# Values and output gate of an mLSTM as one projection of seven block products, in a two-layer hybrid decoder

## The chip, the core and the metric

The kernel runs on one core of a Trainium2 chip. A core has five engines with queues of their own that meet at semaphores: TensorE (matrix products; its weight loads are listed apart as PEld), VectorE (DVE), ScalarE (ACT), GpSimd (POOL) and SyncE (SP), which here only issues loads. DMAs are also issued by POOL, and those of POOL can add to what is already in the destination. Accumulation is in PSUM, eight banks of 128 partitions x 512 numbers; everything else lives in SBUF.

The metric is the device time of one execution in microseconds (us), the median over runs. A measurement here tells a difference of about 0.2% from none.

## What is computed

Two layers over 512 tokens of width 1024. Each has a mixer of two branches and an MLP. Cut to what matters:

```python
def hybrid_layer(x, ...):
    h = rmsnorm(x, norm_mix)
    z = h @ w_in
    q_a, k_a, v_a, q_m, k_m, v_m, o_m, if_m, gates = jnp.split(z, splits, axis=-1)
    q_a = partial_rope(rmsnorm(q_a...)); k_a = partial_rope(rmsnorm(k_a...))
    att = sliding_window_attention(q_a, k_a, v_a, att_sinks)          # 8 heads, 2 key heads, window 128
    hm = mlstm_chunkwise(q_m, k_m, v_m, i_pre, f_pre)                 # 4 heads, values of 128
    hm = rmsnorm(hm, m_head_norm) * jax.nn.sigmoid(o_m)
    g_a, g_m = jnp.split(gates, 2, axis=-1)
    mixed = sigmoid(g_a) * (att @ w_att_branch) + sigmoid(g_m) * (hm @ w_m_branch)
    x = x + mixed @ w_out
    u = relu(rmsnorm(x, norm_ffn) @ w_ff1)
    return x + (u * u) @ w_ff2
```

The edit concerns `v_m` and `o_m`, each `h` (512 x 1024) times 512 columns of `w_in`.

## The kernel before

**Numbers in two parts.** Every operand of a large product is split into a high part (ScalarE copies it into a rounded type) and a low part (VectorE subtracts). `mm3` then makes three matmuls per tile: high by high, high by low, low by high. A group of steps (`group_steps`) computes 512 x 512 outputs: for each 128 rows k of the weight, `chunk` loads a 128 x 512 tile and splits it, and four steps m make three matmuls each into four banks of PSUM. In `feat_steps` the weight is stationary, in `tok_steps` the activation (`acts[k]`, the two parts of the normed, transposed input).

**The order.** The mixer's second half is one list: `weave(fill, side)` (line 819). `fill` is the sequence of projection steps, each a quarter of a unit, so that a group over k = 8 is eight units and one of the branches' groups (k = 4) is four. `side` holds everything else with a place in units: it is traced when the fill reaches that place. Before: the mLSTM's queries and keys (units 0 to 8), gate groups `s0` and `s1` (8 to 24), the values `tok_steps(..., ev_v)` (24 to 32), the attention branch `a_steps(0)`, `a_steps(1)` (32 to 40), gate group `s2` (40 to 48), the output gate `tok_steps(..., ev_o)` (48 to 56), `s3` (56 to 64). Behind the list come the mLSTM's branch on `hmT`, the merge, and `w_out`.

Tracing order is not yet the engines' order: a scheduler puts each engine's instructions into a queue by when they become ready and by priority, and what stands under `tc.high_priority()` (weight loads, their splits, the reading of PSUM) goes ahead. Buffers of one tag are handed out in the order of the trace, though: a tile waits for the release of the one that held its buffer before. Tags that matter: `wraw` (three raw weights), `wh` and `wl` of pool `wsp` (four split weights), `a` of pool `act` (32 tiles of 128 x 512, `slot()`), `t` of pool `tmp` (17, `temp()`), `m` (five banks of PSUM for projections, `bank()`), `aux` (three for everything else), and single ones in `mid`: `mid6` (the attention's values `v2`), `kvi` (its keys), `mid10` (first `kT`, then the mLSTM's values `vm`).

**The side work.** Attention unit i = (block of 128 queries b, key head kv): scores and masks (`att_scores`) at 7 + 1.65 i, softmax (`att_softmax`, exponentials in line 614, scaling in 619) at 1.25 more, transposes, split and POOL's mask (`att_probs`, line 634) at 3.45 more, output at 5.65 more (`att_out`, whose last steps, lines 652 and 653, write block b of `att_acts[2 kv]` and `att_acts[2 kv + 1]`). The last one, i = 7, stands at 24.2. The gates' sigmoids (line 686) follow the reading of their banks; `back` reloads the table of exponentials. mLSTM head h: decay rows (`m_decay`) at 28 + 4.65 h, then four blocks of weights (`m_weights`: exponentials, POOL's mask, a score matmul, a product) and four of outputs (`m_out`, whose matmuls are `aux<-vm,t`). `m_norm` norms all heads, `ev_o` multiplies with the output gate, `head_tr` transposes and splits them into `hmT`.

The MLP of both layers already uses a scheme of seven block products, with sums of activations made by VectorE and sums of weights made by adding DMAs; the mixer's projections are plain.

Of the kernel before, what the change touches and what calls it, by code (L numbers as in the profile page):

```python
# [33 lines left out]
def hybrid_kernel(ctx, tc, x, norm_mix, w_in, att_q_norm, att_k_norm, att_sinks, m_gate_bias,  # L34
# [41 lines left out]
    def temp(dt=F32):  # L76
        return now["tmp"].tile([P, T], dt, tag="t", name=nm("t"))
# [20 lines left out]
    def f32(ap):  # L98
        return ap.bitcast(F32)
# [288 lines left out]
    def mixer(l, norm, late, order, phase):  # L388
# [8 lines left out]
        def wcols(c0, n):  # L397
            return lambda k: [W[k * P:(k + 1) * P, c0:c0 + n]]
# [285 lines left out]
        def sigmoid(tiles):  # L684
            for t in tiles:
                i = sc.activation(t, t, AF.Sigmoid)
            return i

        def back(i):

            with tc.issue_after(i.ins):
                sc.preload_act_table_set(LN_EXP)
# [9 lines left out]

            return sg, feat_steps(acts, wcols(C_G + 512 * g, 512), ev)

        vm = []

        def ev_v(b, ps):
            if b == 0:
# [34 lines left out]
        def m_weights(h, s):  # L743
            cmb = cmbs[h]
            n = (NB - s) * P
            e = wts[h, s] = temp()

            ve.tensor_scalar(e[:, 0:P], cmb[:, s * P:(s + 1) * P], bias[:, s, s, h:h + 1], None, op0=ALU.max)
            sc.activation(e[:, 0:P], e[:, 0:P], AF.Exp, scale=-1.0, bias=bias[:, s, s, h:h + 1])
            for t in range(s + 1, NB):  # L750
                eb = e[:, (t - s) * P:(t - s + 1) * P]
                sc.activation(eb, cmb[:, t * P:(t + 1) * P], AF.Exp, scale=-1.0,
                              bias=bias[:, s, t, h:h + 1])
            gp.affine_select(out=e[:, 0:P], in_=e[:, 0:P], compare_op=ALU.is_ge, fill=0.0,
                             base=0, pattern=[[1, P]], channel_multiplier=-1)
            ps = aux()
            ks = slice(s * P, (s + 1) * P)
            pe.matmul(ps[:, :n], m_k[h][:, ks], m_q[h][:, s * P:], start=True, stop=False)
            pe.matmul(ps[:, :n], m_k[h][:, ks], m_ql[h][:, s * P:], start=False, stop=True)
            ve.tensor_tensor(e[:, :n], e[:, :n], ps[:, :n], op=ALU.mult)  # L760

        def m_out(h, t):
            ps = aux([P, MV + 1])
            for s in range(t + 1):
                pe.matmul(ps, wts[h, s][:, (t - s) * P:(t - s + 1) * P], vm[0][:, s, h, :],
                          start=s == 0, stop=s == t)
            dn = sm([P, 1], "dn")
            ve.scalar_tensor_tensor(dn, ps[:, MV:], -1.0, em[:, t, h:h + 1], op0=ALU.mult, op1=ALU.max)
            ve.tensor_tensor(dn, ps[:, MV:], dn, op=ALU.max)
            ve.reciprocal(dn, dn)  # L770
            hs = hm[t][:, h * MV:(h + 1) * MV]
            sc.activation(hs, ps[:, :MV], AF.Copy, scale=dn)
            sc.activation(ps[:, :MV], hs, AF.Square, accum_out=hss[:, t, h:h + 1])

        def m_norm():
            ve.tensor_scalar(hss, hss, 1.0 / MV, EPS, op0=ALU.mult, op1=ALU.add)
            hr = sm([P, NB, MH], "hr", 1)
            rsqrt(hr, hss, "hq")
            for t in range(NB):
                h3 = hm[t].rearrange("p (h v) -> p h v", h=MH)  # L780
                ve.tensor_tensor(h3, h3, hr[:, t, :].unsqueeze(2).to_broadcast([P, MH, MV]), op=ALU.mult)

        prod = []

# [9 lines left out]
        def ev_o(b, ps):  # L794
            so = temp()
            sc.activation(so, ps, AF.Sigmoid, scale=norm.col[:, b:b + 1])
            ve.tensor_tensor(hm[b], hm[b], so, op=ALU.mult)
            if b == NB - 1:
                sigmoid(g2)

        for h in range(MH):
            at = 28 + 4.65 * h
            side.append((at, lambda h=h: m_decay(h)))
            for i in range(NB):
                side += [(at + 1.75 + 4.65 * i / NB, lambda h=h, i=i: m_weights(h, i)),
                         (at + 4.65 + -0.55 + 4.65 * (i + 0.5) / NB, lambda h=h, i=i: m_out(h, i))]
# [564 lines left out]
```

## Time and profile before

| | |
|---|---|
| device time, median of 3 runs | 1304.13 us (1303.62 to 1304.37) |
| span of the profiled execution | 1302.9 us |
| mean granted TensorE clock over the span | 1.000 |
| bytes moved by DMA | 177.61 MB, mean 136 GB/s |

The profile lists for each engine its busy time as a share of the span. Matmuls are pipelined, so their own durations (about 389 ns for 512 columns) overlap; the distance from one start to the next is what one costs. A line such as L47 is that of the helper through which all matmuls go, so matmuls are told apart by their tiles: `mm<-...` are projections, `aux<-...` attention and mLSTM. Other tiles: `i` parts of the input, `a` a tile of `act`, `t` one of `tmp`, `w`, `wh`, `wl` a weight and its parts.

### The profile page before, as it was taken

To read this page: it belongs to the slowest core of one execution; us is meant where nothing else is said; L and a number is where in the kernel's file an instruction comes from. 1 tells how busy PE (TensorE), PEld (TensorE's weight loads), DVE (VectorE), ACT (ScalarE), POOL (GpSimd) and SP (SyncE) were. 2 spreads that over 40 slices of the span, in tenths; PEclk is the share of its full clock that TensorE was granted. 3 is DMA by queue.
4 is the path that set the end of the run, shared out by engine and by line. 5 is a ranking of instruction groups with operands and counts; after the bars stand their busy time and mean duration, and the time that the engine had idled before them with its cause. 6 is when DMAs were issued, how large, how long until landed. Compare 5 with 4: busy or idle time off the path is not lost. (4 is left out here: it accounts for less than half of the span.)

```text
span 1302.9 us, 19074 instructions
## 1 busy us (share of the span) xinstructions
PE 1291.5 (99%) x6978; PEld 1105.2 (85%) x6978; DVE 955.5 (73%) x1505; ACT 763.7 (59%) x1329; POOL 200.4 (15%) x281
## 2 busy tenths in 40 slices
PE   9999999999999999999999999999999999999998
PEld 6877788888889999999888778888888899999987
DVE  4699754475677897968948996545737878879797
ACT  5578755544466665656555787554445556665563
POOL 4511100000003021131115111000000030311210
PEclk9999999999999999999999999999999999999999
DMA  5422222372369888898124222223714597988953
GB/s 154 110 72 59 74 81 74 90 249 82 98 155 172 236 185 207 195 211 216 33 75 114 65 66 75 79 75 92 256 57 129 141 215 195 201 212 196 213 148 98
DMA packets 130542, 177.61 MB, mean 136 GB/s; under 512 B 9864, under 2 KB 78320, under 8 KB 130448
## 3 DMA queue, kind: packets, MB, share of 16 engines
q1 hardware_dynamic: 94208, 131.82, 32.7%
q0 software_dynamic: 35520, 44.17, 21.2%
q8 instruction: 55, 0.90, 0.3%
q10 hardware_dynamic: 720, 0.40, 0.1%
q14 instruction: 39, 0.32, 0.1%
HBM read 174.27 MB, written 2.10 MB: 135 GB/s over the span
## 5 line engine op out<-in xcount | busy, mean ns | idle before, releaser
L47 PE MATMUL mm<-i,wh 128*128 128x512 f32 (+1 forms) x1280 | 352.7, 362 | 0.0
L867 ACT ACTIVATE wh<-raw 128x1024 fp32r<-128x1024 f32 x212 | 223.1, 1056 | 181.1 <-PE mm L47 114.0
L868 DVE TENSOR_TENSOR wl<-raw,wh 128x1024 fp32r<-128x1024 f32 x212 | 255.2, 1218 | 74.2 <-ACT wh L867 72.3
L47 PEld LDWEIGHTS mm<-i,wh 128*128 128x128 f32 x1280 | 224.3, 189 | 32.1 <-DVE a L699 0.8
L166 DVE TENSOR_TENSOR wl<-w,wh 128x512 fp32r<-128x512 f32 (+1 forms) x208 | 140.8, 679 | 137.7 <-ACT wh L165 129.4
L47 PE MATMUL mm<-i,wl 128*128 128x512 f32 (+1 forms) x640 | 229.8, 360 | 0.0
L165 ACT ACTIVATE wh<-w 128x512 fp32r<-128x512 f32 (+1 forms) x208 | 127.0, 611 | 146.7 <-PE mm L47 122.8
L47 PE MATMUL mm<-wh,uh 128*128 128x512 f32 x440 | 171.8, 390 | 0.0
L47 PE MATMUL mm<-wl,uh 128*128 128x512 f32 x440 | 171.7, 390 | 0.0
L47 PE MATMUL mm<-wh,ul 128*128 128x512 f32 x440 | 171.2, 389 | 0.0
L1027 POOL DMA_DIRECT2D raw<-in_w_ff_dram x48 | 62.3, 1304 | 591.3 <-DMA raw<-in_w_ff_dram 316.9
L47 PE MATMUL mm<-wh,i 128*128 128x512 f32 (+1 forms) x512 | 150.6, 370 | 1.2 <-ACT wh L165 0.6
L47 PEld LDWEIGHTS mm<-i,wl 128*128 128x128 f32 x640 | 120.8, 189 | 18.1 <-DVE wl L868 0.4
L47 PEld LDWEIGHTS mm<-wh,i 128*128 128x128 f32 x512 | 92.0, 188 | 19.0 <-DVE i L179 2.1
L913 DVE SCALAR_TENSOR_TENSOR x<-mm,ms,x 128x512 f32<-128x512 f32 x126 | 90.4, 743 | 9.9 <-PE mm L47 9.9
L47 PEld LDWEIGHTS mm<-wh,ul 128*128 128x128 f32 x440 | 82.6, 188 | 17.4
L47 PEld LDWEIGHTS mm<-wh,uh 128*128 128x128 f32 x440 | 82.8, 188 | 16.1
L47 PEld LDWEIGHTS mm<-wl,uh 128*128 128x128 f32 x440 | 82.8, 188 | 15.6
L47 PE MATMUL mm<-wl,i 128*128 128x512 f32 (+1 forms) x256 | 93.0, 363 | 0.0
L47 PE MATMUL mm<-wh,a 128*128 128x512 f32 x256 | 81.3, 392 | 0.0
L47 PE MATMUL mm<-a,wh 128*128 128x512 f32 x256 | 80.5, 397 | 0.0
L47 PE MATMUL aux<-i,wh 128*128 128x256 f32 x384 | 69.5, 283 | 0.0
(259 smaller groups left out, 2161.0 us busy)
## 6 DMA issues: line engine op xcount, KB each, us to landing
raw<-in_w_ff_dram SPq DMA_DIRECT2D x144, 512.0 KB, 5.2
raw<-in_w_ff_dram POOLq DMA_DIRECT2D x84, 512.0 KB, 7.8
w<-in_w_in_dram SPq DMA_DIRECT2D x128, 256.0 KB, 2.6
w<-in_w_out_dram SPq DMA_DIRECT2D x32, 256.0 KB, 2.7
w<-in_w_att_branch_dram SPq DMA_DIRECT2D x16, 256.0 KB, 2.6
w<-in_w_m_branch_dram SPq DMA_DIRECT2D x16, 256.0 KB, 2.7
w<-in_w_in_dram SPq DMA_DIRECT2D x16, 128.0 KB, 2.1
out_dram<-x SPq DMA_DIRECT2D x7, 256.0 KB, 2.0
```

Of the source, the lines that this page charges most:

```text
L47: latest[0] = nc.tensor.matmul(*args, **kw)
L165: sc.activation(wh[:, :off], raw[:, :off], AF.Copy)
L166: ve.tensor_tensor(wl[:, :off], raw[:, :off], f32(wh[:, :off]), op=ALU.subtract)
L867: sc.activation(hi, src, AF.Copy)
L868: ve.tensor_tensor(lo, src, f32(hi), op=ALU.subtract)
L913: ve.scalar_tensor_tensor(xh[:, cc], ps[i][:, cc], ms[j][:, b:b + 1], xh[:, cc], op0=ALU.mult, op1=ALU.add)
L1027: gp.dma_start(to[h], src(h, i, j), accum_op=ALU.add)
```

## The change

The values and the output gate are no longer two groups of 8 x 4 steps. The activation is seen as two halves of tokens by two halves of k, the weight as two halves of k by two column blocks (output gate, values), and the four 256 x 512 results are made of seven products of 256 x 512 x 512 in the manner of Strassen and Winograd. `vo_step(n, k, i)` is one step of product n: three matmuls for rows k and tokens i of a half.

- Products 1, 2 and 4 take activation quarters as they are; 5, 6, 3 and 7 take sums, made by `sums1`, `sums_next` and `sums3` (nine VectorE operations on 128 x 1024 in the bytes of `mid6` and `kvi`, then splits into `tmp` tiles).
- Products 1 and 2 take weight blocks through `chunk`; the others take weight sums in `wa` (`tmp` tiles, begun at unit 25) and `wb` (`act` tiles), loaded by SP and added to by POOL's DMAs (`more`), 16 of them in a layer.
- Results are read from PSUM in between (`value`, `output`); the output gate's sigmoids follow the last product (`gates_o`) with a table reload behind them, and `m_norm` multiplies with them.
- The order becomes: queries and keys, `s0`, `s1`, `a_steps(0)`, `a_steps(1)` (24 to 32), the seven products (32 to 46), `s2`, `s3` (46 to 62).
- The mLSTM starts at 39.6 instead of 28, with 3.2 units from head to head instead of 4.65; `m_norm` stands at 56.9, `head_tr` at 58.4 + f. The sigmoids of `g2` are traced together with those of `g3`.

```diff
+        def more(r, i, j, k):
+            with tc.high_priority():
+                gp.dma_start(r, block(i, j, k), accum_op=ALU.add)
...
+        def begin(k):
+            wa[k] = temp()
+            load(wa[k], 0, 0, k)
+            more(wa[k], 0, 1, k)
+
+        def weight(n, k):
+            if n in (1, 2):
+                return chunk([block(n - 1, 0, k)])
+            if n == 3:
+                wb[k] = slot()
+                load(wb[k], 1, 1, k)
+            w = parts_of((wb if n in (3, 7) else wa)[k])
+            if n == 5:
+                more(wa[k], 1, 1, k)
+            if n == 6:
+                more(wa[k], 1, 0, k)
+            if n == 3:
+                more(wb[k], 0, 1, k)
+            return w
...
+        def sums1():
+            a, b = (mid.tile([P, 4, H], F32, tag=t, name=nm("sc")) for t in ("mid6", "kvi"))
+            scratch["a"], scratch["b"] = a, b
+            (h10, l10), (h11, l11) = quad(1, 0), quad(1, 1)
+            ve.tensor_tensor(a, h10, l10, op=ALU.add)
+            ve.tensor_tensor(b, h11, a, op=ALU.subtract)
+            ve.tensor_tensor(b, b, l11, op=ALU.add)
+            sum_parts(5, b)
+
+        def sums_next(key, t, i):
+            b = scratch["b"]
+            h, lo = quad(t, i)
+            ve.scalar_tensor_tensor(b, b, -1.0, h, op0=ALU.mult, op1=ALU.subtract)
+            ve.tensor_tensor(b, b, lo, op=ALU.subtract)
+            sum_parts(key, b)
...
-            sc.activation(vm[0][:, b, :, 0:MV], ps.rearrange("p (h v) -> p h v", h=MH), AF.Copy,
-                          scale=norm.col[:, b:b + 1])
...
+        def gates_o():
+            for b in range(NB):
+                last = sc.activation(so[b], so[b], AF.Sigmoid, scale=norm.col[:, b:b + 1])
+            back(last)
+
+        plan = {5: ("y", None, [(value, 1, True)]), 1: ("x", (0, 0), [(output, 0, True)]),
+                3: ("y", None, [(value, 0, True)]), 6: ("x", None, [(value, 0, False)]),
+                2: ("f", (0, 1), [(output, 0, False)]), 7: ("x", None, [(value, 1, False), (output, 1, True)]),
+                4: ("f", (1, 1), [(output, 1, False)])}
...
+        def vo_step(n, k, i):
+            which, at, outs = plan[n]
+            fresh = n in (5, 1, 2, 4) and k == 0
+            if fresh and i == 0:
+                held[which] = [bank(), bank()]
+            if i == 0:
+                ready[0] = weight(n, k)
+            if at:
+                c = slice(H * at[0] + i * P, H * at[0] + (i + 1) * P)
+                ah, al = (a[:, c] for a in acts[4 * at[1] + k])
+            else:
+                ah, al = (a[:, k % 2, i * P:(i + 1) * P] for a in sums[n][k // 2])
+            mm3(held[which][i], ah, al, ready[0][0], ready[0][1], fresh, False, skip_group_check=True)
...
+        vo_steps = [(0.25, lambda n=n, k=k, i=i: vo_step(n, k, i))
+                    for n in (5, 1, 3, 6, 2, 7, 4) for k in range(4) for i in range(2)]
...
+                ve.tensor_tensor(hm[t], hm[t], so[t], op=ALU.mult)
...
+        side += [(25.0 + 0.5 * k, lambda k=k: begin(k)) for k in range(4)]
+        side += [(25.0, sums1), (28.5, lambda: sums_next(6, 0, 0)), (31.5, lambda: sums_next(3, 0, 1)), (36.5, sums3)]
+        pace = 3.2
         for h in range(MH):
-            at = 28 + 4.65 * h
+            at = 39.6 + pace * h
...
-        side.append((28 + 4.65 * (MH + 1) + -0.55, m_norm))
+        side.append((56.9, m_norm))
         g2, s2 = gate_steps(2)
-        g3, s3 = gate_steps(3, lambda: back(sigmoid(g3)))
+        g3, s3 = gate_steps(3, lambda: back(sigmoid(g2 + g3)))
...
-        side += [(57.75 + 1.25 * f, lambda f=f: head_tr(f)) for f in range(MH)]
-        weave(feat_steps(acts, wcols(C_QM, 512), ev_qk) + s0 + s1 + tok_steps(acts, wcols(C_VM, 512), ev_v)
-              + a_steps(0, g0) + a_steps(1, g1) + s2 + tok_steps(acts, wcols(C_OM, 512), ev_o) + s3, side)
+        side += [(58.4 + 1.0 * f, lambda f=f: head_tr(f)) for f in range(MH)]
+        weave(feat_steps(acts, wcols(C_QM, 512), ev_qk) + s0 + s1 + a_steps(0, g0) + a_steps(1, g1) + vo_steps
+              + s2 + s3, side)
```

More of the change, by code (lines that the diff above doesn't have):

```diff
@@ new lines, in parts_of @@
+        def parts_of(r):
+            with tc.high_priority():
+                wh, wl = (now["wsp"].tile([P, T], F32R, tag=t, name=nm(t)) for t in ("wh", "wl"))
+                sc.activation(wh, r, AF.Copy)
+                ve.tensor_tensor(wl, r, f32(wh), op=ALU.subtract)
+            return wh, wl
+        def begin(k):
[16 more added lines that the diff above has]
+            return w
@@ new lines, in quad, with sum_parts @@
+        def quad(t, i):
+            return [f32(g[:, :, H * t:H * (t + 1)]) for g in norm.groups[i]]
+        def sum_parts(key, src):
+            sums[key] = [split(src[:, 2 * p:2 * p + 2, :], get=lambda: now["tmp"].tile([P, 2, H], F32R, tag="t", name=nm("t")))
+                         for p in range(2)]
+        def sums1():
[6 more added lines that the diff above has]
+            sum_parts(5, b)
@@ new lines, in output @@
+        def output(t, ps, first):
+            for i in range(2):
+                if first:
+                    so.append(slot())
+                    sc.activation(so[-1], ps[i], AF.Copy)
+                else:
+                    ve.tensor_tensor(so[2 * t + i], so[2 * t + i], ps[i], op=ALU.add)
+        def gates_o():
[6 more added lines that the diff above has]
+                4: ("f", (1, 1), [(output, 1, False)])}
@@ new lines, in mixer @@
+        held, ready = {}, {}
+        def vo_step(n, k, i):
[8 more added lines that the diff above has]
+                ah, al = (a[:, c] for a in acts[4 * at[1] + k])
+            else:
+                ah, al = (a[:, k % 2, i * P:(i + 1) * P] for a in sums[n][k // 2])
+            mm3(held[which][i], ah, al, ready[0][0], ready[0][1], fresh, False, skip_group_check=True)
+            if k == 3 and i == 1:
+                with tc.high_priority():
+                    for f, t, first in outs:
+                        f(t, held[which], first)
+                if n == 4:
+                    gates_o()
```

37 lines of the change are left out of this document (26 added, 11 removed).

## The prediction

> **What bounds the kernel now.** I read the page first, then the chain of waits, then busy time by stretches of the second layer's mixer, and last the timeline of each engine in the 20 us in which the edit takes work away.
>
> ```profile
> span 1302.9 us, 19074 instructions
> ...
> PE 1291.5 (99%) x6978; PEld 1105.2 (85%) x6978; DVE 955.5 (73%) x1505; ACT 763.7 (59%) x1329; POOL 200.4 (15%) x281
> ...
> PEclk9999999999999999999999999999999999999999
> ```
>
> From the chain (start, length, what), and from the stretches (stretch, its length, then each engine's busy time and instructions):
>
> ```profile
> 872.67 20.50 PE mm L47 x90
> ```
>
> ```profile
> core 0: us, PE busy (x) PEld busy (x) DVE busy (x) ACT busy (x) POOL busy (x), PEclk, DMA share, GB/s
> ...
> 136.00:152.00 16.00, 16.00 (x75) 12.80 (x74) 12.55 (x31) 13.76 (x39) 2.91 (x4) 1.00 0.23 68
> 716.00:781.40 65.40, 62.63 (x317) 48.68 (x317) 60.34 (x150) 51.76 (x141) 9.90 (x17) 1.00 0.24 65
> 781.40:797.60 16.20, 16.20 (x75) 12.96 (x74) 12.65 (x33) 13.92 (x40) 2.91 (x4) 1.00 0.23 66
> 808.30:862.50 54.20, 54.20 (x279) 46.10 (x278) 29.19 (x89) 29.89 (x91) 4.36 (x13) 1.00 0.27 77
> ```
>
> TensorE is idle for 11.4 us of 1302.9, so a matmul removed is time removed, and a wait of TensorE is time added. Busy time does not say what a matmul costs, since they overlap; the chain of waits does: 90 in 20.50 us, 0.228 us each. One unit of the woven program (four steps of three matmuls) is 2.73 us. Up to 781.4 us the attention runs beside the first 24 units, and there VectorE is busy 60.34 of 65.40 us: the attention is behind its places in the list, and what is left of it is done in the next 16 us, in which ScalarE is busy 13.92. Layer one shows the same (136 to 152).
>
> That stretch is where the edit acts. Columns: start, length, engine, line, operation, out<-in, shapes, count, idle before.
>
> ```profile
> 781.21 0.39 PE L47 MATMUL mm<-i,wl 128*128 128x512 f32 x1
> 781.43 0.39 PE L47 MATMUL mm<-wh,i 128*128 128x512 f32 x1
> ...
> 789.95 0.63 PE L52 MATMUL aux<-ident,t 128*128 128x128 f32 x4
> 790.33 1.17 PE L47 MATMUL aux<-t,v 128*128 128x512 f32 x4
> ```
>
> ```profile
> 782.26 1.66 ACT L686 ACTIVATE a<-a 128x512 f32<-128x512 f32 x3
> 784.35 0.63 ACT L165 ACTIVATE wh<-w 128x512 fp32r<-128x512 f32 x1 [0.43 <-PE mm L47]
> 785.00 1.28 ACT L692 ACT_TABLE_LOAD   x1
> 786.30 0.40 ACT L614 ACTIVATE t<-t,m 128x128 f32<-128x128 f32 x1
> ...
> 787.12 0.63 ACT L165 ACTIVATE wh<-w 128x512 fp32r<-128x512 f32 x1
> ...
> 790.08 0.61 ACT L165 ACTIVATE wh<-w 128x512 fp32r<-128x512 f32 x1
> ...
> 795.78 0.63 ACT L165 ACTIVATE wh<-w 128x512 fp32r<-128x512 f32 x1 [0.73 <-PE mm L47]
> ```
>
> ```profile
> 791.93 1.00 POOL L634 TENSOR_SCALAR_AFFINE_SELECT t<-t 128x512 fp32r<-128x512 f32 x1 [11.60 <-ACT t L175]
> 793.16 2.11 POOL L634 TENSOR_SCALAR_AFFINE_SELECT t<-t 128x512 fp32r<-128x512 f32 x3 [0.23 <-DVE t L176]
> ```
>
> ```profile
> 789.12 0.68 DVE L619 TENSOR_TENSOR t<-t,den 128x512 f32<-128x512 f32 x1
> ...
> 797.31 0.49 DVE L653 TENSOR_TENSOR a<-t,a 128x128 fp32r<-128x128 f32 x2 [0.17 <-ACT a L652]
> ```
>
> The second gate group ends at 781.43, where the values' projection (stationary `i`) takes over. The seventh attention unit (block 3, first key head) is then still before its softmax: its exponentials start at 786.30, behind the last sigmoids and a table load, line 619 scales them at 789.12, its transposes follow at 789.95, its masks on POOL at 791.9 and 793.2, and its pair of attention parts is complete at about 797.6. TensorE never notices, because 96 matmuls of the values fill the gap.
>
> **The change part by part, for one layer.**
>
> *Matmuls.* Values and gate take 2 x 8 x 4 x 3 = 192 matmuls of 512 columns; seven products take 7 x 4 x 2 x 3 = 168. 24 x 0.228 = **-5.5 us**. Nothing else leaves TensorE.
>
> *The branch behind the first gates.* At unit 24 stands now `a_steps(0)`. Its first matmul needs `att_acts[0]` for all four blocks, hence the seventh unit's parts. Could TensorE do something else meanwhile? The weight parts live in four buffers in program order, so the first branch group holds all four; no later product can be prepared. The new product's sums take the bytes of `v2`, which the last attention unit reads; the mLSTM's tiles come after those. So TensorE waits. When are the parts ready? Before: 797.6. The values' weight passes on ScalarE fall away (784.35 with its wait: 1.08 us to 785.00; 787.12 and 790.08: about 0.53 each, since neighbours overlap by 0.1; the one at 795.78: 0.7): 797.6 - 2.8 = 794.8. From 781.43 that is 13.4 us, of which TensorE works on two sets of transposes (0.38 us from 789.95 to the next row) and two attention outputs (four matmuls of 0.228, 0.91): 2.6. **+10.8 us**. Bounds: no speeding-up, 797.6 - 781.4 - 2.6 = 13.6; and from below, if the softmax started right behind the last sigmoid (783.9, without even a table load) and ran as it did from 786.30 on, less the 2.8: 797.6 - 2.4 - 2.8 = 792.4, 11.0 - 2.6 = 8.4. The second branch pair (eighth unit) is needed 24 matmuls later, 5.5 us, and comes about 2 us later: no wait.
>
> *The clock.* Between 781.8 and about 788 nothing is there for TensorE: over 6 us. What happens then is seen at the program's two ends only:
>
> ```profile
> 1.22 2.93 PE L47 MATMUL aux<-ones 128*128 128x256 f32 x6 [1.22 <-POOL ones L108]
> 5.01 0.94 PE L47 MATMUL aux<-ones 128*128 128x128 f32 x6
> 1298.00:1299.00 1.00, 0.89 (x4) 0.39 (x3) 0.39 (x2) 0.00 (x0) 0.00 (x0) 1.00 0.00 0
> 1301.00:1302.00 1.00, 0.00 (x0) 0.00 (x0) 0.00 (x0) 0.00 (x0) 0.00 (x0) 0.89 0.13 45
> 1302.00:1303.00 1.00, 0.00 (x0) 0.00 (x0) 0.00 (x0) 0.00 (x0) 0.00 (x0) 0.50 0.03 8
> ```
>
> The granted clock falls to 0.50 some 3 us after the last matmul, and the first six matmuls take 2.93 us for 256 columns each, where later six of 128 take 0.94: work is slow from 1.22 to some point between 4.15 and 5.01; I take 3.7 us. If the wait costs the clock, the first 3.7 us behind it run at half speed: 1.8 lost; and one set of transposes and the last output matmuls in the chain take twice as long: 0.6. **+2.4 us**; bounds 0 (the short attention bursts keep it up) and 3.6 (slow for two such times).
> By the Trainium skill (TensorE: Matmul & The Clock Gate, part 1, "The HAM clock gate") one idle window of about 3.4 us halves the clock and about 3.4 us of work restores it, and its advice is to leave no gap over some 3 us between bursts; by that figure the loss is an estimated 1.7 instead of 1.8, and the change breaks the advice twice. The rows at the two ends agree; no gap in the middle of this run is long enough to show it.
>
> *More weights, sums and DMAs.* 28 weight tiles are split instead of 16, 9 operations on 128x1024 and 8 splits of 128x512 make the sums, and 16 loads of 256 KB come with 16 adding DMAs on POOL's queue.
>
> ```profile
> L868 DVE TENSOR_TENSOR wl<-raw,wh 128x1024 fp32r<-128x1024 f32 x212 | 255.2, 1218 | 74.2 <-ACT wh L867 72.3
> L166 DVE TENSOR_TENSOR wl<-w,wh 128x512 fp32r<-128x512 f32 (+1 forms) x208 | 140.8, 679 | 137.7 <-ACT wh L165 129.4
> L1027 POOL DMA_DIRECT2D raw<-in_w_ff_dram x48 | 62.3, 1304 | 591.3 <-DMA raw<-in_w_ff_dram 316.9
> raw<-in_w_ff_dram POOLq DMA_DIRECT2D x84, 512.0 KB, 7.8
> ```
>
> VectorE: 9 x 1.22 + (8 + 12) x 0.68 = 24.6 us, and ScalarE 20 x 0.63 = 12.6; both lie beside 22 units of 2.73 us, 60 us, where VectorE was busy a good half (29.19 of 54.20). POOL: 16 x 1.3 = 21 us at most, in a stretch where it was busy 4.36 of 54.20. An adding DMA of twice the size lands in 7.8 us; each is needed a product or more (8 steps, 5.5 us) later, most two. Queued behind them on POOL are the mLSTM's masks, and at units 25 to 26.5 the attention's last masks. I take **0**; bounds 0 and 3 us (one adding DMA in the way of the masks and one late weight).
>
> *The mLSTM later and closer.* Its last output moves from unit 50.1 to 56.25, and the branch that reads it from 64 to 62.
>
> ```profile
> 864.64 0.48 PE L47 MATMUL mm<-wh,i 128*128 128x512 f32 x1
> ...
> 867.49 0.83 PE L47 MATMUL aux<-vm,t 128*128 128x129 f32 x6
> ...
> 871.61 1.05 PE L47 MATMUL aux<-vm,t 128*128 128x129 f32 x8
> ```
>
> ```profile
> 893.17 0.44 PE aux L52 x4
> ```
>
> ```profile
> 879.81 1.89 DVE L781 TENSOR_TENSOR a<-a,hr 128x512 f32<-128x512 f32 x3
> ...
> 894.37 0.75 DVE L179 SCALAR_TENSOR_TENSOR a<-aux,gcol,a 128x512 fp32r<-128x512 f32 x1 [2.10 <-ACT a L178]
> ```
>
> Unit 48 starts at 864.64 and the last output at 871.61; less 0.6 for the outputs at 867.49 (to the next fill matmul) that is 2.3 units on: 50.3, so it is hardly late. From its end (872.7, where the chain goes on with 90 fill matmuls) to normed heads (881.7) are 9.0 us; four more products by `so`, 0.63 each, 2.5; transposes and split, from 893.17 to 895.12, 1.9: 13.4, with the lateness 0.2 x 2.73 = 0.5 it is 13.9. Cover: 5.75 units, 15.7 us. It just fits; with heads at a distance of 3.2 units in place of 4.65 the lateness grows. **+0.5 us**; bounds 0 and 4 (the heads one unit and a half later).
>
> *Sum.* -5.5 + 10.8 + 2.4 + 0 + 0.5 = +8.2 a layer, +16.4 for two. On the profiled execution's 1302.9 that is 1319.3; its span lies 1.2 under the runs' median of 1304.13, so the forecast is **1320.5 us**.
>
> **The rivals.**
>
> *The attention is ready in time (faster).* It is late in part because ScalarE and VectorE prepare the values' weights; freed of them it might finish almost at the gates' end, and only the 24 matmuls would count: 1304.1 - 11.0 = 1293.1. It decides where the parts come before 781.4 + 2.6 + 5.5 = 789.5. Against it: the exponentials started at 786.30 behind sigmoids that remain, and 11.3 us of chain follow, of which 2.8 are weights. Chance 0.08.
>
> *The adding DMAs set the pace.* If three products of each layer wait once for a landing of 7.8 us less 5.5 of cover and the masks of the last attention units wait for a landing too, 2 x (3 x 2.3 + 7.8) = 29 more: 1350. For it: POOL works in order, and the page's row of line 1027 shows 316.9 us of POOL waiting for landings; against: few other things stand in POOL's queue there. Chance 0.06.
>
> *The mLSTM's end becomes the bound.* Heads a third closer, with 2 weights a unit beside them and one more pair of table loads (1.28 us, the row at 785.00): a wait of 7 us ahead of the last branch in each layer in place of 0.5, 1333. Against: ScalarE was busy 29.89 of 54.20 with heads at 4.65. Chance 0.09.
>
> **How the numbers follow.** Forecast 0.75, with its own bounds: low 2 x (-5.5 + 8.4 + 0 + 0 + 0) = +5.8, 1310; high, with wait 13.6, clock 3.6, DMAs 1 and tail 2, 2 x 14.7 = +29.4, 1333.5. Between them all terms at their ends at once are unlikely. The range runs from 1307 to 1336, which leaves out the faster rival, the DMA rival and a little of the forecast, about 0.2. Under 0.2% (2.6 us) a measurement of this kernel can't tell a change from none. Faster 0.09 (the first rival and a trifle), within 0.02, slower 0.89.
>
> **What would show it.** Right: in each mixer a gap of TensorE of some 10 us between the second gates' last matmul and the first with the branch's weights, ended by `a` of line 653 (some lines lower), a granted clock under 1 in it, and 48 matmuls fewer in all. The gap absent, or filled by sums or products, makes the forecast wrong; a granted clock of 1.00 there takes 4.8 off; TensorE waiting on a DMA or on head splits ahead of the last branch speaks for the second or third rival.

## The result, and the profile after

The changed kernel takes 1324.91 us (median of 4 runs, 1323.33 to 1325.47), the kernel before 1304.14 beside it: a ratio of 1.016, with a 95% interval of 1.0145 to 1.0174. That is 20.8 us slower, 10.4 in each layer, against a forecast of 1320.5 us.

From the page of the kernel after:

```profile
span 1323.6 us, 19221 instructions
...
PE 1290.8 (98%) x6930; PEld 1097.9 (83%) x6930; DVE 1011.8 (76%) x1581; ACT 798.0 (60%) x1385; POOL 227.9 (17%) x313
...
PEclk9999899999999999999999998999999999999999
```

TensorE has 48 matmuls fewer, and its busy time is almost what it was (1290.8 against 1291.5). VectorE has 56 us more work. In two places, the middle of each mixer, the granted clock falls.

The timeline of TensorE in layer two (start, length, engine, line, operation, out<-in, shapes, count, idle before and what ended it):

```profile
791.25 0.39 PE L47 MATMUL mm<-i,wl 128*128 128x512 f32 x1
798.35 1.08 PE L52 MATMUL aux<-ident,t 128*128 128x128 f32 x4 [6.72 <-DVE t L619]
...
805.96 1.32 PE L47 MATMUL mm<-a,wh 128*128 128x512 f32 x5
...
840.57 0.73 PE L47 MATMUL mm<-wh,t 128*128 128x512 f32 x2 [1.40 <-ACT wh L723]
...
857.00 0.50 PE L47 MATMUL mm<-wh,i 128*128 128x512 f32 x1 [0.86 <-ACT wh L165]
...
921.42 0.30 PE L52 MATMUL aux<-ident,a 128*128 128x128 f32 x1 [0.89 <-DVE a L901]
...
932.13 0.62 PE L47 MATMUL mm<-a,wh 128*128 128x512 f32 x2
```

The first row is the last matmul of the second gates, the one at 805.96 the first of the attention's branch, the one at 932.13 the first of the mLSTM's. So the branch begins 14.5 us behind the end of the gates (791.25 + 0.23 = 791.48). TensorE stands still for the first 6.7 us of that, then does the two sets of transposes and the outputs of the attention's last units, with waits between them. Behind the branch come gaps that were not there before: ahead of product 3 (840.57), inside product 2, ahead of its last row of weights (857.00), and ahead of the heads' transposes (921.42).

What ScalarE does meanwhile:

```profile
792.31 1.65 ACT L686 ACTIVATE a<-a 128x512 f32<-128x512 f32 x3
793.98 1.28 ACT L692 ACT_TABLE_LOAD   x1
795.27 0.40 ACT L614 ACTIVATE t<-t,m 128x128 f32<-128x128 f32 x1
```

A table load (from 789.96), four sigmoids, of which the first row shows three, a table load back, then the seventh unit's exponentials, 3.8 us behind the gates' end (before: 4.9). Busy time by stretches (stretch, length, each engine's busy time and instructions, granted clock, DMA share, GB/s):

```profile
138.10:148.30 10.20, 5.53 (x17) 4.64 (x18) 6.71 (x19) 7.71 (x28) 2.34 (x4) 0.50 0.17 52
...
791.48:805.96 14.48, 7.25 (x24) 5.62 (x24) 10.65 (x28) 11.43 (x35) 3.44 (x5) 0.76 0.13 37
...
798.30:803.20 4.90, 4.85 (x16) 4.10 (x17) 3.10 (x8) 3.04 (x10) 1.77 (x3) 0.50 0.19 49
...
810.00:832.00 22.00, 22.00 (x99) 18.22 (x98) 20.91 (x30) 8.45 (x15) 6.03 (x7) 1.00 0.77 158
```

The first row is layer one, the others layer two. The clock is 0.50 for some 10.2 us in layer one and while the attention's pieces run in layer two. In the branch (810 to 832) it is full again, TensorE has no gap, and VectorE is busy 95% of the time.

### The profile page after: what moved, and what is told of

It is laid out like the page before. It is cut to its first block, busy times and chain, and to the rows that moved or that the text cites. A ratio compares the mean times of both kernels' runs of the same rounds, so it can differ in the third digit from the quotient of the medians.

```text
span 1323.6 us, 19221 instructions
## 1 busy us (share of the span) xinstructions
PE 1290.8 (98%) x6930; PEld 1097.9 (83%) x6930; DVE 1011.8 (76%) x1581; ACT 798.0 (60%) x1385; POOL 227.9 (17%) x313
## 5 line engine op out<-in xcount | busy, mean ns | idle before, releaser
L166 DVE TENSOR_TENSOR wl<-w,wh 128x512 fp32r<-128x512 f32 (+1 forms) x192 | 129.2, 676 | 106.9 <-ACT wh L165 103.9
L165 ACT ACTIVATE wh<-w 128x512 fp32r<-128x512 f32 (+1 forms) x192 | 116.9, 610 | 125.3 <-PE mm L47 94.2
L1143 POOL DMA_DIRECT2D raw<-in_w_ff_dram x48 | 62.2, 1303 | 545.7 <-DMA raw<-in_w_ff_dram 370.1
L47 PE MATMUL mm<-wh,i 128*128 128x512 f32 (+1 forms) x352 | 100.7, 360 | 2.6 <-ACT wh L165 2.3
L47 PEld LDWEIGHTS mm<-wh,i 128*128 128x128 f32 x352 | 61.9, 188 | 14.2 <-ACT wh L165 3.3
L1300 POOL DMA_DIRECT2D raw<-in_w_ff_dram x36 | 44.1, 1224 | 149.4 <-DVE wl L984 100.9
```

Source lines behind the costliest of these rows:

```text
L47: latest[0] = nc.tensor.matmul(*args, **kw)
L165: sc.activation(wh[:, :off], raw[:, :off], AF.Copy)
L166: ve.tensor_tensor(wl[:, :off], raw[:, :off], f32(wh[:, :off]), op=ALU.subtract)
L1143: gp.dma_start(to[h], src(h, i, j), accum_op=ALU.add)
L1300: gp.dma_start(to[h], src(h, i, j), accum_op=ALU.add)
```

## The experiments

The theory after the result was: the attention's end, no longer covered, costs some 10 us per layer, and the products give back what their 24 missing matmuls win. All times below are medians beside runs of the kernel before on the same chip (1303.65 to 1303.96).

**The order alone.** The kernel before with the branch moved, and plain projections.

```diff
-        weave(feat_steps(acts, wcols(C_QM, 512), ev_qk) + s0 + s1 + tok_steps(acts, wcols(C_VM, 512), ev_v)
-              + a_steps(0, g0) + a_steps(1, g1) + s2 + tok_steps(acts, wcols(C_OM, 512), ev_o) + s3, side)
+        weave(feat_steps(acts, wcols(C_QM, 512), ev_qk) + s0 + s1 + a_steps(0, g0) + a_steps(1, g1)
+              + tok_steps(acts, wcols(C_VM, 512), ev_v) + s2 + tok_steps(acts, wcols(C_OM, 512), ev_o) + s3, side)
...
-            at = 28 + 4.65 * h
+            at = 36 + pace * h        # pace 3.2
```

> The kernel before, with its two plain projections, but the attention branch right behind the second gates, the values behind it, and the mLSTM's heads from unit 36 at a distance of 3.2; no sums, no adding DMAs, 192 matmuls as before. Theory (the wait for the attention's end costs the time, 10.3 us a layer with the slow clock in it): 1304.1 + 20.6 = 1325, between 1321 and 1329, and a gap of TensorE of 6 to 7 us in each mixer, ended by line 619. Rival (the seven products with their sums and adding DMAs cost it, the order little): under 1310.

1322.98 us, a ratio of 1.0148 (1.0132 to 1.0163). TensorE in layer two:

```profile
789.60 0.39 PE L47 MATMUL mm<-i,wl 128*128 128x512 f32 x1
...
796.70 1.09 PE L52 MATMUL aux<-ident,t 128*128 128x128 f32 x4 [6.72 <-DVE t L619]
...
804.38 0.96 PE L47 MATMUL mm<-a,wh 128*128 128x512 f32 x3
...
930.41 0.61 PE L47 MATMUL mm<-a,wh 128*128 128x512 f32 x2
```

The same gap, to the hundredth, and the branch again 14.6 us behind the gates' end (789.83). So the order makes the slowdown, 19.3 us of it. The second thing to read is the stretch from one branch to the other: 804.38 to 930.41 is 126.03 us here, 805.96 to 932.13 is 126.17 after, although after has 24 matmuls less in it, 5.5 us. The seven products win nothing: 5.6 us are lost behind the branch in this layer. In layer one it is 126.71 us after against 125.90, so 6.3 there.

**Sigmoids later.** The sigmoids of the gates traced behind the last attention unit.

```diff
-        g1, s1 = gate_steps(1, lambda: back(sigmoid(g0 + g1)))
+        g1, s1 = gate_steps(1)
+        side.append((24.3, lambda: back(sigmoid(g0 + g1))))
```

> The changed kernel, but the eight sigmoids of the first two gate groups are traced behind the last attention output, at ordinary priority. Theory (the wait is ScalarE's chain: the seventh unit's exponentials stand behind four sigmoids and a table load and could start some 3 us sooner, at 792.4 instead of 795.3): 2.8 us a layer less, 1324.9 - 5.6 = 1319.3. Rival (VectorE's or POOL's part of the chain, or the clock, sets the end): 1324 to 1326.

1333.75 us. ScalarE in layer two:

```profile
785.60 1.28 ACT L614 ACT_TABLE_LOAD   x1
791.90 1.28 ACT L686 ACT_TABLE_LOAD   x1
```

A later place in the trace didn't put the sigmoids behind the exponentials: without their priority they were spread among them, each change costing a table load (two of six in this mixer are shown). So the run does not answer its question.

**Sigmoids held back.** The same intent with an explicit order. The sigmoids are again those of the first two gate groups, not the output gate's, as the expectation has it.

```diff
-                sc.activation(dh, b3[:, j, :], AF.Copy)
+                last_att[0] = sc.activation(dh, b3[:, j, :], AF.Copy)
...
+        def late_sigmoids():
+            with tc.issue_after(last_att[0].ins):
+                i = sigmoid(g0 + g1)
+            back(i)
+
+        side.append((24.3, late_sigmoids))
```

> Kernel after, with the output gate's sigmoids held until ScalarE has issued the last copy of the attention's last unit. Theory (the branch waits for ScalarE's exponentials, which stand behind four sigmoids and a table load, about 3 us): the last exponentials run some 3 us sooner after the gates' end, TensorE's gap of 6.7 us falls to about 4, and both layers together win 5.6 us: 1319.3 us (1317.5 to 1321.5). Rival (the chain's later links, VectorE's weights and GpSimd's masks, are held by their own work and not by ScalarE): the gap stays at 6 to 7 us and the time at 1324 to 1327, or more where the sigmoids then delay the first products' readings.

1326.88 us. The profiled execution took 1331.10, the other three 1326.44 to 1326.99. TensorE, then ScalarE (lines from 638 on stand two further down than in the kernel after):

```profile
799.93 0.63 PE L52 MATMUL aux<-ident,t 128*128 128x128 f32 x4 [3.37 <-DVE t L619]
...
806.71 1.33 PE L47 MATMUL mm<-a,wh 128*128 128x512 f32 x5
...
840.98 0.50 PE L47 MATMUL mm<-wh,i 128*128 128x512 f32 x1 [2.71 <-ACT wh L165]
...
937.92 0.62 PE L47 MATMUL mm<-a,wh 128*128 128x512 f32 x2
```

```profile
840.29 0.63 ACT L165 ACTIVATE wh<-w 128x512 fp32r<-128x512 f32 x1 [3.54 <-DMA w<-in_w_in_dram]
```

The gap did halve, from 6.72 to 3.37 us, and the branch begins 10.3 us behind the gates' end (796.39) instead of 14.5: the four sigmoids with their table loads in front of the exponentials were that much of the wait. But the time did not fall. The stretch from branch to branch grew from 126.17 to 131.21 us, in this execution, which was 4 us longer than the others: the sigmoids now take ScalarE from 809 to 817, and in the products after that TensorE waits for weights, 2.71 us of it inside product 1, where ScalarE itself awaits a load for 3.54. That the sigmoids' new place made the load late is not shown; why it left late was not followed further.

**TensorE kept busy.** 26 products of ones into a spare bank behind the second gates, so that the clock stays up.

```diff
+        def keep():
+            ps = bank()
+            for _ in range(26):
+                pe.matmul(ps[:, :2 * P], ones, ones.unsqueeze(1).to_broadcast([P, 2, P]), start=True, stop=True)
...
-        weave(feat_steps(acts, wcols(C_QM, 512), ev_qk) + s0 + s1 + a_steps(0, g0) + a_steps(1, g1) + vo_steps
+        weave(feat_steps(acts, wcols(C_QM, 512), ev_qk) + s0 + s1 + [(0, keep)] + a_steps(0, g0) + a_steps(1, g1) + vo_steps
```

> The changed kernel with 26 matmuls of ones by ones into the spare PSUM bank right behind the second gates, about 6 us that nothing reads. Theory (the granted clock halves in the gap, and the attention's transposes and outputs then take twice as long): the clock stays at 1.00, matmuls of the attention 232 ns apart instead of 427, 2.7 us a layer less, 1324.9 - 5.4 = 1319.5. Rival (the slow matmuls lie beside ScalarE's and VectorE's steps, so that the branch starts as late as before): 1324 to 1326; later than that if the added matmuls run past the transposes.

1334.96 us. Its stretches (the first three are layer one's product 3 and the wait ahead of it), then TensorE, then ScalarE:

```profile
186.80:188.40 1.60, 0.02 (x1) 0.00 (x0) 0.01 (x1) 0.63 (x1) 0.00 (x0) 1.00 0.95 279
188.40:189.30 0.90, 0.89 (x3) 0.46 (x4) 0.68 (x1) 0.18 (x1) 0.00 (x0) 1.00 0.97 364
189.30:192.70 3.40, 3.40 (x9) 2.64 (x10) 2.69 (x4) 2.34 (x4) 2.79 (x4) 0.50 0.62 104
...
786.00:812.00 26.00, 25.42 (x126) 21.58 (x125) 20.49 (x48) 17.97 (x51) 5.02 (x9) 1.00 0.20 52
```

```profile
802.69 0.60 PE L52 MATMUL aux<-ident,t 128*128 128x128 f32 x4
...
806.27 3.18 PE L47 MATMUL mm<-ones 128*128 128x256 f32 x14
809.11 0.81 PE L47 MATMUL mm<-a,wh 128*128 128x512 f32 x2
...
849.91 0.73 PE L47 MATMUL mm<-wh,t 128*128 128x512 f32 x2 [3.06 <-ACT wh L723]
```

```profile
808.09 0.51 ACT L652 ACTIVATE a<-t 128x128 fp32r<-128x128 f32 x2 [0.96 <-DVE t L649]
```

The clock stays at 1.00 up to the branch, and yet the branch starts only 0.7 us sooner behind the gates' end (13.8 us against 14.5). That is the least that the slow clock costs, not all of it: the dummy products took about 11 us of TensorE instead of 6 (52 records, 34 of them in the 7.34 us from 795.35 to 802.69), so that they themselves stood ahead of the transposes and, the last 14 records of them, ahead of the branch, whose operand ScalarE had written by 808.60. From the transposes to that operand it took 5.9 us here; in the kernel after 7.6 from the transposes to the branch. So the half clock cost between 0.7 and 1.7 us of the wait, and the rest of it lay beside waits for ScalarE and VectorE. The loss came later, as waits for weights, such as the 3.06 us ahead of product 3. That the dummy products caused them by pushing the attention's last output back is likely, but no run shows it apart. Behind these waits the clock is halved among full matmuls, in layer one for 3.40 us, of which half is lost: 1.7 us, by my estimate.

**Product 2 ahead of the branch.** Its operands are plain blocks, so 24 matmuls (5.5 us) can cover part of the wait; its result is held in the free tiles of `q_tok` until product 1 adds to it.

```diff
-        weave(feat_steps(acts, wcols(C_QM, 512), ev_qk) + s0 + s1 + a_steps(0, g0) + a_steps(1, g1) + vo_steps
+        weave(feat_steps(acts, wcols(C_QM, 512), ev_qk) + s0 + s1 + vo_steps(2) + a_steps(0, g0) + a_steps(1, g1)
+              + vo_steps(5, 1, 3, 6, 7, 4)
```

> The changed kernel with product 2, which takes the input and a weight block as they are, moved from sixth place to right behind the second gates, ahead of the attention branch; its result waits in the idle tiles of the queries. Theory (24 matmuls fill 5.5 us of the gap, and what is left of it is too short to slow the clock): 5.5 + 2.7 = 8.2 us a layer less, 1324.9 - 16.4 = 1308.5. Rival (its weights and readings delay the attention's end as much as it fills): 1318 or more; if only the clock stays slow, 1314.

1317.82 us, 7.1 less than after. TensorE, then ScalarE:

```profile
798.02 1.09 PE L52 MATMUL aux<-ident,t 128*128 128x128 f32 x4 [5.07 <-DVE t L619]
```

```profile
794.96 0.40 ACT L614 ACTIVATE t<-t,m 128x128 f32<-128x128 f32 x1
```

5.5 us of cover take only 1.65 us off the gap. The gates end at 787.4 here, so the exponentials start 7.6 us behind them instead of 3.8: the moved product brings the readings of its weights and of its result to ScalarE in front of the sigmoids and the exponentials. The rest of the win lies behind the branch, where the stretch to the mLSTM's branch is some 1.2 us shorter than after, the 24 moved matmuls counted. Cover that uses the engine of the chain it covers is worth less than its length.

**Where the 5.6 us among the products go.** Three runs: the shared weights `wb` of products 3 and 7 loaded two products sooner; VectorE's sums left out; the adding DMAs left out.

```diff
-            if n == 3:
+            if n == 5:
                 wb[k] = slot()
                 load(wb[k], 1, 1, k)
```

```diff
+            if not at:
+                at = {5: (0, 0), 3: (1, 1), 6: (1, 0), 7: (0, 1)}[n]
...
-        side += [(25.0, sums1), (28.5, lambda: sums_next(6, 0, 0)), (31.5, lambda: sums_next(3, 0, 1)), (36.5, sums3)]
```

```diff
         def more(r, i, j, k):
-            with tc.high_priority():
-                gp.dma_start(r, block(i, j, k), accum_op=ALU.add)
+            pass
```

> Kernel after, with the weights that products 3 and 4 share allocated and loaded two products sooner. Theory (the gap of 1.40 us ahead of product 3 in layer 2, and 1.75 in layer 1, is the late issue of that load, which stands in SP's queue behind other loads): the gaps go, 1.4 to 1.75 us per layer, 1321.5 us (1320.5 to 1322.5). Rival (ScalarE's reading of the weights is late for ScalarE's own work, or the wait moves to the next product): 1324 to 1326.

> Kernel after without VectorE's sums of the activations' quarters: products 5, 3, 6 and 7 take quarters as they are, so the output isn't the reference's. Theory (the new small waits among the products, some 5 us per layer, come of VectorE, which is busy 95% of the time there): 3 to 4.5 us per layer go, 1317 us (1315 to 1319.5). Rival (they come of the weights' loads and ScalarE's readings of them, which this leaves alone): 1322 to 1325.5.

> Kernel after without the adding DMAs, so that products take weight blocks that are not summed, and the output isn't the reference's; VectorE's sums stay. Theory that VectorE makes the small waits: the adding DMAs cost nothing, 1323.5 to 1326 us, but for what GpSimd's masks of the attention win. Rival (the adding DMAs make the weights late): up to 2.5 us per layer go, 1320 us (1318.5 to 1322).

Sooner weights: 1318.41 us, 6.5 less than after. No sums: 1325.18, no change. No adding DMAs: 1319.89, 5.0 less. (The runs without sums and without adding DMAs compute something else than the layer.) Without the sums VectorE is idle half the time in the branch, and the wait ahead of product 3 stays (a stretch, and TensorE):

```profile
810.00:832.00 22.00, 22.00 (x99) 18.22 (x98) 11.65 (x18) 6.66 (x11) 4.03 (x6) 1.00 0.67 126
```

```profile
840.34 0.73 PE L47 MATMUL mm<-wh,i 128*128 128x512 f32 x2 [1.79 <-ACT wh L723]
```

So my theory that the full VectorE makes the small waits fell: 95% busy, and yet its sums cost nothing. The weights make them. SyncE's queue (SPq) in the kernel after, what its loads wait for from 800 to 860 us (us in total, times, longest), and the same loads in the run with sooner weights:

```profile
817.11 19.73 SPq L155 DMA_DIRECT2D w<-in_w_in_dram  x6
836.89 1.85 SPq L714 DMA_DIRECT2D a<-in_w_in_dram  x4
```

```profile
SPq L155 <- DVE wl L166: 43.3, 12, 12.4
```

```profile
815.56 3.54 SPq L714 DMA_DIRECT2D a<-in_w_in_dram  x4
```

The loads of line 714 for product 3 leave at 836.89, behind six loads of line 155, which take 19.73 us to leave because they wait for VectorE's split of an earlier tile (line 166) to free one of the three raw buffers; ScalarE can read product 3's weights only then, and product 3 starts at 840.57. Loaded sooner they leave at 815.56, the gap is gone and the stretch from branch to branch is 123.48 us (801.95 to 925.43) in place of 126.17. The win of 6.5 is more than the two gaps (1.40 and 1.75): smaller waits went with them. The adding DMAs are the other part: without them the stretch is 124.31 (801.76 to 926.07), and the gap inside product 2 is gone, while one ahead of product 3 stays. The two wins add to 11.5 us, about what is lost in both layers, but they were not taken out in one run, so how far they overlap is open.

**No wait at all.** The branch reads four tiles of the normed input in place of the attention's outputs.

```diff
-            return feat_steps(att_acts, lambda k: [w_att_branch[l, k * P:(k + 1) * P, 512 * g:512 * g + 512]],
+            return feat_steps(acts[:4], lambda k: [w_att_branch[l, k * P:(k + 1) * P, 512 * g:512 * g + 512]],
```

> Kernel after, with the branch's products reading four tiles of the layer's normed activations in place of the attention's outputs, so that they wait for nothing of the attention; the output isn't the reference's, and all instructions stay. Theory (the branch's wait for the attention's end costs 10.3 us per layer, 14.5 us less 4.2 us of TensorE's work inside it, half clock included): TensorE goes straight on after the gates, its clock stays full, and 20.6 us go: 1304.3 us (1301 to 1308). Rival (what the wait hid comes back as other waits, as where TensorE was kept busy: weights and evictions late among the products): 1311 to 1318.

1329.55 us: slower than after, beyond even the rival. TensorE in product 5 (which begins at 819.70) and its clock there, ScalarE, VectorE, POOL:

```profile
827.80 1.22 PE L47 MATMUL mm<-wh,t 128*128 128x512 f32 x2 [5.28 <-ACT wh L723]
...
828.00:836.00 8.00, 7.00 (x16) 5.07 (x17) 7.36 (x11) 4.23 (x8) 2.63 (x3) 0.50 0.50 75
```

```profile
826.08 1.15 ACT L175 ACTIVATE t<-sc 128x512 fp32r<-128x512 f32 x2 [7.31 <-DVE sc L767]
827.13 0.61 ACT L723 ACTIVATE wh<-t 128x512 fp32r<-128x512 f32 x1
828.30 0.63 ACT L723 ACTIVATE wh<-t 128x512 fp32r<-128x512 f32 x1 [0.56 <-DMA t<-in_w_in_dram]
```

```profile
811.81 1.23 DVE L758 TENSOR_TENSOR sc<-i,i 128x1024 f32<-128x1024 f32 x1
...
824.76 1.22 DVE L767 TENSOR_TENSOR sc<-sc,i 128x1024 f32<-128x1024 f32 x1
```

```profile
820.23 3.52 POOL L718 DMA_DIRECT2D t<-in_w_in_dram  x4 [7.33 <-DVE wl L724]
```

The attention's end has a second customer. The sums use the bytes of the attention's values, so they begin behind its last unit (811.81), and product 5 needs them. With the branch first in line and waiting, they have its 22 us to get done in; with the branch no longer waiting, product 5 is reached sooner and stands for 5.28 us at its second row of weights. Two things hold that row there, and the trace does not tell which alone would. ScalarE is idle for 7.31 us ahead of the splits of product 6's sums, because VectorE has not made them (824.76), and product 5's weight readings stand behind in its queue. But the weights come hardly sooner: POOL issues four adding DMAs only from 820.23 on, after waiting for VectorE's split of the first row (line 724), and ScalarE waits for such a DMA again at its next reading (0.56 us). The profile's chain of waits goes through one of these DMAs (6.90 us from 821.32). So the sums that cost nothing in the kernel after, or the adding DMAs, or both, are on the path here. Behind the gap come 8 us at a clock of 0.50, with TensorE busy 7.00 of them; half of that, 3.5 us, is my estimate of what the clock adds.

So the 10 us are not won by freeing the branch alone. What the run shows is that an attention that ends late also holds what follows. That only work which needs neither can cover it is an inference; the next runs agree with it.

**Both edits, then more cover.** Product 2 ahead and weights sooner together; then also half of the third gates (48 matmuls on 256 of their columns) ahead of the branch, with the heads closer still and the sums four units later; the diff is that of the second against the first, cut.

```diff
+        s2a, s2b = (feat_steps(acts, wcols(C_G + 1024 + 256 * i, 256), ev_2, ms=2) for i in range(2))
...
-        weave(feat_steps(acts, wcols(C_QM, 512), ev_qk) + s0 + s1 + vo_steps(2) + a_steps(0, g0) + a_steps(1, g1)
+        weave(feat_steps(acts, wcols(C_QM, 512), ev_qk) + s0 + s1 + vo_steps(2) + s2a + a_steps(0, g0) + a_steps(1, g1)
               + vo_steps(5, 1, 3, 6, 7, 4)
-              + s2 + s3, side)
+              + s2b + s3, side)
...
-            at = 39.6 + pace * h      # pace 3.2
+            at = 41.5 + pace * h      # pace 2.6
```

> Kernel after, with product 2 right behind the second gates and the shared weights loaded two products sooner: the two edits that won 7.1 and 6.5 us alone. Theory (they remove different waits): 1311.3 us (1309.5 to 1313). Rival (product 2's weights were among the late loads that the sooner load helped, so that the gains overlap): 1314 to 1317.

> As the kernel with both edits, and half of the third gates' projection (48 matmuls, 11 us) also moved ahead of the branch, the mLSTM's heads closer still, the activations' sums four to five marks later. Theory (16.4 us of work now cover the attention's last chain, which took 14.5 to 18 us after the second gates): TensorE's gap falls below 2 us and its clock stays full, some 16 to 18 us less than after in all by the wait alone and with the sooner load 1303 us (1299 to 1308), level with before. Rival (half of the gates no longer covers the mLSTM's end, whose heads then decide): gap ahead of the heads' transposes over 3 us per layer, 1310 us or more.

Both: 1314.11 us, 10.8 less than after where the single wins add to 13.6, so the gains overlap, as the rival had it. The gap stands, 5.06 us. With more cover: 1309.29 us, without any gap ahead of the branch, and a little over the range. This kernel's first head takes the values of two of its four blocks before product 7's part is in them, so its time is not that of the whole layer. Its last mLSTM heads are not the bound (a gap of 0.96 us ahead of their transposes); a load seems to stand in the way again. In the last kernel the heads therefore begin 0.7 units later, so that they read whole values, and the shared weights are to be loaded beside product 1, behind its own:

```diff
             if n in (1, 2):
-                return chunk([block(n - 1, 0, k)])
-            if n == 5:
-                wb[k] = slot()
-                load(wb[k], 1, 1, k)
+                w = chunk([block(n - 1, 0, k)])
+                if n == 1:
+                    wb[k] = slot()
+                    load(wb[k], 1, 1, k)
+                return w
...
-            at = 41.5 + pace * h
+            at = 42.2 + pace * h
```

> Product 2 and half of the third gates' projection ahead of the branch, as in the run with more cover, but the mLSTM's heads begin 0.7 of a mark later, so that every head reads whole values (there the third and fourth blocks of the first head were taken before product 7's part was in them), and the shared weights are loaded beside product 1, behind its own weights and no longer ahead of them. Theory (with the attention's wait covered, what is left are late weights: the gap of 1.3 us per layer ahead of product 1, whose fourth load stood behind the shared weights' loads, goes; the heads' later start costs nothing that shows): 1306.5 us (1304.5 to 1309), still level with before or a little slower. Rival (the heads' end is the bound now): 1310 us or more, with a gap over 2 us ahead of the heads' transposes.

1304.18 us (12 runs, 1303.29 to 1308.79) beside 1303.88: a ratio of 1.0007 (0.9999 to 1.0016), level with before. A stretch from the gates to the branch and one inside the products, then TensorE and SyncE's queue, of an execution that took 1307.23:

```profile
782.70:803.10 20.40, 20.35 (x93) 16.30 (x92) 16.04 (x44) 17.20 (x50) 2.98 (x4) 1.00 0.36 110
...
838.20:841.60 3.40, 3.40 (x9) 2.63 (x8) 3.34 (x6) 1.87 (x4) 2.63 (x3) 0.50 0.53 90
```

```profile
837.15 0.50 PE L47 MATMUL mm<-wh,i 128*128 128x512 f32 x1 [1.35 <-ACT wh L165]
```

```profile
824.70 1.75 SPq L714 DMA_DIRECT2D a<-in_w_in_dram  x4
829.81 8.37 SPq L155 DMA_DIRECT2D w<-in_w_in_dram  x4
```

From the second gates' end to the branch TensorE is now busy 20.35 of 20.40 us at a full clock, and all of the change's 20.8 us are won back. But the gap inside product 1 is still 1.35 us, not gone as the theory had it. The edit did not do what it was to do: the shared weights' four loads (824.70) still leave ahead of product 1's fourth (the first of the four at 829.81). So this run is no test of that theory, though its time came out just under the range; what made the difference to the run before may be the heads' new place. Behind the gap this execution has 3.40 us at a clock of 0.50. A kernel with 48 matmuls fewer, 11 us, that only draws level still loses about as much elsewhere; no version here was faster than before.

## Why the prediction was right, and where it was off

*The matmuls, -5.5 a layer.* 48 went, as said. That they are 5.5 us of path in each layer rests on their distance in the chain, and the run of the order alone fits: there, with 24 more in the stretch, 126.03 us leave no room for the waits that the products show. The term itself was not measured apart from them.

*The wait, +10.8, and the clock, +2.4.* Place, cause and chain were right. The moment was predicted at 13.4 us behind the gates' end plus 0.6 for slow pieces, and was 14.5. The work that TensorE does meanwhile was taken at 2.6 us; there are 15 matmuls of 512 columns and two sets of transposes, 15 x 0.228 + 2 x 0.38 = 4.2. So the two terms together are 14.5 - 4.2 = 10.3, not 13.2. The predicted releaser, `a` of line 653, was not that of the long gap: it ends with line 619, because the seventh unit's own transposes wait there, and only then come the outputs.

*The clock by itself* was the step that failed in its mechanism. It did fall to 0.50. But I put 1.8 of the 2.4 us on the branch's first matmuls, and these ran at full clock: the slow time was over by then. It fell on the attention's pieces, for which the prediction had 0.6: with the clock kept up, the branch came 0.7 us sooner, and its operand at most 1.7. By the Trainium skill (TensorE: Matmul & The Clock Gate, part 1, "The HAM clock gate") an idle window of about 3.4 us halves the clock; the gap of 6.7 us agrees, but in the run that kept TensorE busy the clock was halved 0.9 us after a gap of 1.6 us, where that rule gives no loss.

*Weights, sums and DMAs, 0.* This was the term of the sum that was mis-sized: from branch to branch the products lost 5.6 us in layer two, of which 0.9 is the gap ahead of the heads' transposes and 4.7 belong here, over the bound of 3. The sums cost nothing in the kernel after, as predicted, if not for the reason given ("busy a good half" became 95%). What I had left out is SyncE's queue: I counted the loads, but not what stands before them in their queue. Sooner loads alone won 6.5 us in both layers together. The adding DMAs were priced at 0 with one late weight as the bound; leaving them out won 5.0.

*The mLSTM's tail, +0.5.* A gap of 0.89 us, ahead of the heads' transposes as described.

*The sum.* -5.5 + 10.3 + 4.7 + 0.9 = 10.4 a layer, as measured, where 8.2 was predicted: the wait was 2.9 us too dear and the products 4.7 too cheap, so that two errors met halfway. That the time came out so near is partly luck. The fit to a tenth is too: the terms are those of layer two, and by the same 10.3 the run of the order alone would have been 20.6 us slower, where it was 19.3. None of the rivals came true: the attention was not ready in time, the mLSTM's end did not become the bound, and the adding DMAs cost 5.0 us and not 29.

## What to carry to other kernels

When a chain of small steps on other engines ends beside a long projection, that projection is doing a job; before moving it, measure how far behind the chain runs (here 14.5 us) and name the work that will stand there instead, which must not load the same engine. A busy share doesn't tell who is waited for: VectorE at 95% cost nothing, while four loads in each layer, in the wrong place of a queue, cost 6.5 us in all. So ask of a late weight when its load left, and read in the trace whether an edit moved it. And a wait that several customers share can't be priced by freeing one of them: another takes it over, here at 5.28 us.

## What the runs showed of the hardware

The granted clock is halved for short stretches even after short gaps: 1.6 us idle, 0.9 us of matmuls at 1.00, and then 3.4 us at 0.50 with TensorE busy throughout, in the run that kept TensorE busy; 3.40 us at 0.50 behind a gap of 1.35 us in the last kernel. It does not follow every such gap: in the kernel after, it stayed at 1.00 behind gaps of 1.40 and 1.75 us. Of the twelve executions of the last kernel, the seven with a mean clock of 1.000 took 1303.29 to 1304.66 us, and the five with 0.997 to 0.999 took 1306.01 to 1308.79. After a gap of 6.7 us the slow stretch lasted about 10.2 us in layer one while the attention's pieces kept TensorE busy 5.53 of 10.20 us.
